# A prompt and sample step of a hybrid layer on one core: idle matmuls at the start, the second layer norm's steps and the samples' sums at other places, and another tail

## The chip, the cores and the metric

The kernel runs on one core of a Trainium2 chip. The metric is the device time of one execution in microseconds (us); lower is better. The kernel before was timed three times: 2386.88, 2387.24 and 2389.86 us, median 2387.24. In the text, PE is TensorE (matmuls), DVE is VectorE, ACT is ScalarE, POOL is GpSimd and SP is SyncE, which here issues most DMAs.

## The reference, cut to what matters

One layer is computed for 2048 prompt tokens and for 64 sample tokens (8 sequences of 8, each with a state of its own). Model width is 1024, the feed-forward width 4096, all in float32.

```python
proj = einsum('btd,dp->btp', x, w_in)                      # 1024 -> 3584
q, f_pre, i_val, g, gate_b, gate_c, h = split(proj, SPLITS)
o, s_new = _hgrn2(silu(q), log_f, k, i_val, s_hgrn)        # 4 heads of 128, chunks of 64
o = o * rsqrt(mean(o * o) + RMS_EPS) * onorm_g * silu(g)
yc = gate_b * conv3(gate_c * h)
mix = einsum('btm,md->btd', concat([o, yc]), w_out)
x = layer_norm(ALPHA * x + mix, ln1_g, ln1_b)
hid = square(relu(einsum('btd,df->btf', x, w_ff1)))        # 1024 -> 4096
x = layer_norm(ALPHA * x + einsum('btf,fd->btd', hid, w_ff2), ln2_g, ln2_b)
```

The outputs are the new tokens of prompt and samples (`y` and `ys`), the heads' states and the last two rows of the convolution's input.

## The kernel before

Matmuls are made in a format with a shorter mantissa. So that the result is as exact as float32, each operand is split into a high part, copied by ACT, and a low part, the difference, made by DVE (L165 for activations, L210 for weights), and each product is three matmuls: high by high, high by low, low by high. The low half isn't made at once: `split` and `unit_split` put it into a list `later`, which `flush` empties, so that DVE's subtraction comes after ACT's copy has been issued. Weights come as units of 128 x 1024 values. SP's queue loads them in the order of use, through three staging buffers `st`, into four pairs `wh`/`wl`; `weights(u)` hands out a unit and splits the ones ahead.

The prompt is worked off in four blocks of 512 tokens, b=0 to 3; the 64 samples go with block 1. A block has these stages, in this order on PE:

- the projections and heads, 56 steps i=0 to 55 (the loop at L862): i=0 to 15 the heads' projections, i=16 to 31 those whose result has tokens on its partitions, i=32 to 55 the convolution's. After each step `rec_step` issues a piece of the heads' recurrence. It is a chain between the engines: DVE builds products and decays (L613, L614, L620, L634, L640), PE makes sums and scores from them (L644, L645, L683, L699), and DVE copies these to their places (L603, L686, L693). A piece comes in the middle of the projections, and on PE its matmuls stand in line with theirs.
- the output projection and the first layer norm.
- the feed-forward part, in two rounds of a first and a second product. It is arranged in the manner of Strassen's method, so that fewer products are needed. In block 0, 64 and later more sums of weight quarters are made by DMAs that POOL issues (`make_sums`, L347 and L349); POOL is started on them by a small addition `tick` (L354). In the second product, the results leave the banks of PSUM by DVE (`add_to`, L1242 and L1245), queued in a list `slow`, one or two of which go into `later` with each unit.
- in block 1, the samples' part of the second product is summed by `sample_sums`. A bank holds two halves of 64 rows; ACT copies the upper one to the lower rows (`upper`, L256), DVE adds the two (L1252), and a third operation adds the sum to the samples' rows (L1259, L1261). The copy and L1252 are issued where `sample_sums` is called, behind the matmuls of that unit, and the third goes into `slow`.

A block's second layer norm is not made at its end. For each tile of 128 tokens (64 for the samples) `layer_norm2` gives three steps, put in a list `bg`: a1, the statistics (L266 twice, L269, L270) and a power by POOL (L271) for one over the deviation; a2, which subtracts the mean and multiplies by the weight (L287); a3, which multiplies by the power, adds the bias (L290) and has POOL store the tile (L291). `pump()` issues the next step of the list. The loop over the next block's 56 steps calls it:

```python
        for i, _ in enumerate(main()):
            rec_step()
            ...
            if i % 2 == 0:
                pump()
        while bg:
            pump()
```

The last block has no next one. Its last part is finished tile by tile (L1374): for each of four tiles PE makes two banks of 512 columns, 12 matmuls each; DVE adds each bank to the tile and takes the statistics, POOL the power; `scaled` (L1363 by DVE, L1364 by ACT) and `stored` (L1370 by DVE, L1371 by POOL, and a DMA) finish the tile before it. The last tile has lines of its own (L1390 to L1398).

What sets the order: each engine takes its instructions in the order in which the program issues them, and waits at each for its operands and buffers. DVE's order is therefore the order of the calls, `flush` and `pump` above.

Of the kernel before, what the change touches and what calls it, by code (L numbers as in the profile page):

```python
# [13 lines left out]
AF = mybir.ActivationFunctionType  # L14
# [3 lines left out]
P = 128  # L18
# [6 lines left out]
NS = 64  # L25
# [36 lines left out]
def hybrid_step(ctx, tc, a, o):  # L62
# [67 lines left out]
    def load_constants():  # L130
        nc.sync.dma_start(small, a["small"])
        nc.sync.dma_start(ident, a["ident"])
        nc.sync.dma_start(mask_f, a["masks"])
        nc.sync.dma_start(smask, a["smask"])
        g.memset(nhalf, -0.5)
        g.memset(halo, 0.0)
        g.memset(ones.bitcast(F32), 1.0)
# [115 lines left out]
    def upper(bank):  # L253

        tmp = TMP().rearrange("p a b -> p (a b)")
        s.activation(tmp[:NS], bank[NS:2 * NS, :], AF.Copy)  # L256
        return tmp[:NS]
# [140 lines left out]
    for _ in range(6):  # L398
        unit_dma()
    load_constants()  # L400
    carry = None


    for b in range(NB):
# [452 lines left out]
        def main():  # L857
            yield from m1()
            yield from m2()
            yield from m3()  # L860

        for i, _ in enumerate(main()):  # L862
            rec_step()
            if b == 0 and i >= 6:
                if i == 6:

                    hold(ks[0][:, 0:1])
                next(making, 0)
                next(making, 0)
            if b == 1 and i % 2 == 0:  # L870
                next(making1, 0)
            if i >= 16 and i % (3 if samp else 4) == 0:
                rec_step()
            if i % 2 == 0:
                pump()
        while bg:
            pump()
# [370 lines left out]

        def sample_sums(bank, into):

            up = upper(bank)
            v.tensor_tensor(up, up, bank[:NS, :], ALU.add)  # L1252

            def add(dh, sign):
                z = x1[NC][:NS, dh * 512:dh * 512 + 512]
                op = ALU.add if sign > 0 else ALU.subtract
                if (NC, dh) in touched:
                    v.tensor_tensor(z, z, up, op)
                else:  # L1259
                    touched.add((NC, dh))  # L1260
                    v.scalar_tensor_tensor(z, z, ALPHA, up, ALU.mult, op)  # L1261

            for dh, sign in into:
                slow.append(lambda dh=dh, sign=sign: add(dh, sign))
# [87 lines left out]
        if b == NB - 1:  # L1352

            c = NCH - 1
            ws = [weights(u) for u in pl["last"]]
            flush_all()
            h, l = last

            sts = [SM((P, 17)) for _ in range(nt)]

            def scaled(t):
                st = sts[t]
                v.scalar_tensor_tensor(st[:, 16:17], st[:, 12:13], -1.0, st[:, 15:16], ALU.mult, ALU.mult)  # L1363
                s.activation(x1[t], x1[t], AF.Identity, scale=st[:, 15:16], bias=st[:, 16:17])  # L1364

            def stored(t):
                for dh in range(2):
                    ds_ = slice(dh * 512, dh * 512 + 512)
                    z = x1[t][:, ds_]
                    v.tensor_tensor(z, z, lnb[:, 0, ds_], ALU.mult)  # L1370
                    g.tensor_tensor(z, z, lnb[:, 1, ds_], ALU.add)  # L1371
                    nc.sync.dma_start(dst(t)[:, ds_], z)

            for t in range(nt):  # L1374
                for dh in range(2):
                    bank = PS()
                    for i in range(FC):
                        slot, cs = 2 * (i // 2) + t // 2, slice(t % 2 * P, t % 2 * P + P)
                        rh, rl = (x[:, (i % 2) * 512:(i % 2 + 1) * 512] for x in ws[2 * dh + i // 2])
                        mm3(bank, h[:, slot, i % 2, cs], l[:, slot, i % 2, cs], rh, rl, i == 0, i == FC - 1)  # L1380
                    if t > 0:
                        if dh == 0:
                            scaled(t - 1)
                        else:
                            stored(t - 1)
                    add_to(t, dh, bank, 1)
                    ln_half(sts[t], x1[t], P, dh)
                ln_rstd(sts[t], P)
            t, st = nt - 1, sts[nt - 1]
            v.scalar_tensor_tensor(st[:, 16:17], st[:, 12:13], -1.0, st[:, 15:16], ALU.mult, ALU.mult)  # L1390
            lo, hi = x1[t][:, :512], x1[t][:, 512:]
            s.activation(lo, lo, AF.Identity, scale=st[:, 15:16], bias=st[:, 16:17])
            v.scalar_tensor_tensor(hi, hi, st[:, 12:13], lnb[:, 0, 512:], ALU.subtract, ALU.mult)
            v.scalar_tensor_tensor(hi, hi, st[:, 15:16], lnb[:, 1, 512:], ALU.mult, ALU.add)
            nc.sync.dma_start(dst(t)[:, 512:], hi)
            v.tensor_tensor(lo, lo, lnb[:, 0, :512], ALU.mult)
            v.tensor_tensor(lo, lo, lnb[:, 1, :512], ALU.add)
            nc.scalar.dma_start(dst(t)[:, :512], lo)  # L1398
        for t in range(nt):
            bg.extend(layer_norm2(x1[t], tsz[t], dst(t)))  # L1400
        x1 = x1g = x1h = x1l = None
# [85 lines left out]
```

## Time and profile before

| | |
|---|---|
| median of three runs | 2387.24 us |
| the profiled execution | 2390.55 us |
| its span | 2388.3 us |
| PE busy | 2340.0 us |
| DVE busy | 1785.6 us |
| ACT busy | 1233.5 us |
| POOL busy | 184.9 us |
| mean granted clock of PE | 0.994 |
| idle time of PE ahead of the first product's `X` | 6.69 us |
| last matmul's end to the end of the span (2379.1 to 2388.3) | 9.2 us |

How to read it: rows give the start and duration in us, the engine, the line, the operation, the tiles out and in (`out<-in`, with buffer numbers left out), their shapes, and how many instructions stand in the row; in brackets the idle time of the engine just before, and which engine's tile and line ended it. A window's row gives its bounds and length, then the busy time of PE, the weight load, DVE, ACT and POOL (with counts), the granted clock of PE, the busy share of the DMA engines, and GB/s. The granted clock is 1.00 at full speed.

By start times, the heads' stage begins at about 612 us in block 1, 1260 in block 2 and 1821 in block 3; the step i=32 of block 3 lies at 1924 us.

### The profile page before, as it was taken

How to read it: one execution, taken by the hardware profiler on the slowest of the kernel's cores; microseconds unless marked ns; L12 is line 12 of the kernel's file. 1: busy time of each engine (PE TensorE's matmuls, PEld its weight loads, DVE VectorE, ACT ScalarE, POOL GpSimd, SP SyncE). 2: the span in 40 equal slices, each digit the busy share in tenths (PEclk: the TensorE clock that was granted, in tenths of full speed). 3: DMA queues.
4: the chain of work that ended last, by engine and by line, in shares of the span. 5: the costliest groups of instructions: out<-in, count | busy, mean ns of one | idle time of the engine just before them, and what ended most of it. 6: DMA issues, size and time to landing. Idle time of an engine off the chain costs nothing.

```text
span 2388.3 us, 38146 instructions
## 1 busy us (share of the span) xinstructions
PE 2340.0 (98%) x15036; PEld 2043.1 (86%) x15036; DVE 1785.6 (75%) x2832; ACT 1233.5 (52%) x1922; POOL 184.9 (8%) x234
## 2 busy tenths in 40 slices
PE   8999999999999999999999999999999999999998
PEld 7778978988879889879878788998988788998996
DVE  7856858578785677875688956888588975888678
ACT  5324645565423446646654234665665324665563
POOL 2230021100101110000000000000000001000001
PEclk9999999999999999999999999999999999999999
DMA  8997598867633644545553325456665325456663
GB/s 285 264 282 214 151 266 273 257 200 211 163 107 78 172 149 133 168 150 177 177 177 109 99 71 194 155 187 197 192 210 163 102 79 172 141 176 203 200 191 119
DMA packets 131507, 418.89 MB, mean 175 GB/s; under 512 B 13376, under 2 KB 17856, under 8 KB 131328
## 3 DMA queue, kind: packets, MB, share of 16 engines
q1 hardware_dynamic: 108880, 347.96, 45.7%
q0 software_dynamic: 22016, 67.71, 11.5%
q8 instruction: 118, 1.93, 0.3%
q10 hardware_dynamic: 432, 0.79, 0.1%
q14 instruction: 61, 0.50, 0.1%
HBM read 405.36 MB, written 69.77 MB: 199 GB/s over the span
## 4 chain that ended last, share of the span: by engine, by line
PE 50%; DVE 5%; DMA 1%; issue 1%; ACT 1%; POOL 0%; POOLq 0%; DVEq 0%; ACTq 0%
PE ps L247 9%; PE ps L245 9%; PE ps L246 9%; PE ps L239 6%; PE ps L240 6%; PE ps L241 6%; DVE wl L210 1%; DMA st<-in_w_ff 1%; PE ps L683 1%; PE ps L250 1%; PE ps L251 1%; DVE S L603 0%; DMA st<-T_b 0%; DVE l L165 0%; ACT wh L203 0%
## 5 line engine op out<-in xcount | busy, mean ns | idle before, releaser
L210 DVE TENSOR_TENSOR wl<-st,wh 128x1024 fp32r<-128x1024 f32 x580 | 707.4, 1221 | 173.3 <-ACT wh L203 171.2
L203 ACT ACTIVATE wh<-st 128x1024 fp32r<-128x1024 f32 x581 | 612.9, 1055 | 352.1 <-PE ps L247 125.6
L239 PE MATMUL ps<-X,wh 128*128 128x256 f32 (+2 forms) x1376 | 466.6, 339 | 9.8 <-ACT X L164 8.3
L240 PE MATMUL ps<-X,wh 128*128 128x256 f32 (+2 forms) x1376 | 456.8, 332 | 0.3 <-DVE X L165 0.3
L241 PE MATMUL ps<-X,wl 128*128 128x256 f32 (+2 forms) x1376 | 456.3, 332 | 0.0
L247 PE MATMUL ps<-wh,l 128*128 128x512 f32 x868 | 340.8, 393 | 9.0 <-DVE l L165 8.6
L245 PE MATMUL ps<-wh,h 128*128 128x512 f32 x868 | 338.2, 390 | 0.0
L246 PE MATMUL ps<-wl,h 128*128 128x512 f32 x868 | 338.0, 389 | 0.0
L239 PEld LDWEIGHTS ps<-X,wh 128*128 128x128 f32 x1376 | 263.0, 191 | 35.0 <-ACT X L164 9.3
L241 PEld LDWEIGHTS ps<-X,wl 128*128 128x128 f32 x1376 | 262.8, 191 | 22.0
L240 PEld LDWEIGHTS ps<-X,wh 128*128 128x128 f32 x1376 | 263.2, 191 | 21.3 <-DVE X L165 1.5
L247 PEld LDWEIGHTS ps<-wh,l 128*128 128x128 f32 x868 | 162.9, 188 | 52.4 <-DVE l L165 19.0
L246 PEld LDWEIGHTS ps<-wl,h 128*128 128x128 f32 x868 | 163.0, 188 | 34.0
L245 PEld LDWEIGHTS ps<-wh,h 128*128 128x128 f32 x868 | 163.0, 188 | 33.1 <-ACT h L164 0.4
L165 DVE TENSOR_TENSOR l<-raw,h 128x512 fp32r<-128x512 f32 x217 | 148.2, 683 | 9.8 <-ACT h L164 9.8
L247 PE MATMUL ps<-X,wl 128*128 128x256 f32 (+1 forms) x528 | 152.1, 288 | 0.2 <-DVE wl L210 0.2
L246 PE MATMUL ps<-X,wh 128*128 128x256 f32 (+1 forms) x528 | 151.9, 288 | 0.0
L245 PE MATMUL ps<-X,wh 128*128 128x256 f32 (+1 forms) x528 | 151.9, 288 | 0.0
L271 POOL TENSOR_TENSOR sm<-sm,nhalf 128x1 f32<-128x1 f32 (+1 forms) x34 | 34.7, 1020 | 1475.8 <-DVE sm L270 1429.6
L1147 DVE TENSOR_TENSOR raw<-raw,ps 128x512 f32<-128x512 f32 (+1 forms) x112 | 61.0, 571 | 104.9 <-PE ps L247 104.7
L164 ACT ACTIVATE h<-raw 128x512 fp32r<-128x512 f32 x217 | 133.7, 616 | 2.3 <-PE ps L246 2.2
L239 PE MATMUL ps<-wh,X 128*128 128x512 f32 x256 | 105.8, 413 | 2.8 <-DVE S L603 2.8
(259 smaller groups left out, 4369.2 us busy)
## 6 DMA issues: line engine op xcount, KB each, us to landing
st<-in_w_ff SPq DMA_DIRECT2D x227, 512.0 KB, 3.7
st<-T_b SPq DMA_DIRECT2D x124, 512.0 KB, 3.7
st<-in_w_in SPq DMA_DIRECT2D x110, 512.0 KB, 3.9
st<-T_a SPq DMA_DIRECT2D x88, 512.0 KB, 3.5
st<-in_w_out SPq DMA_DIRECT2D x56, 512.0 KB, 4.5
T_b<-in_w_ff POOLq DMA_DIRECT2D x48, 512.0 KB, 14.7
T_a<-in_w_ff POOLq DMA_DIRECT2D x36, 512.0 KB, 19.1
T_b<-T_b POOLq DMA_DIRECT2D x16, 512.0 KB, 12.9
```

The costliest lines, as they stand in the source:

```text
L164: s.activation(hi, src, AF.Copy)
L165: later.append(lambda: v.tensor_tensor(lo, src, hi.bitcast(F32), ALU.subtract))
L203: s.activation(wh, st, AF.Copy)
L210: v.tensor_tensor(wl, st, wh.bitcast(F32), ALU.subtract)
L239: te.matmul(out, lh, rh, start=first, stop=False)
L240: te.matmul(out, lh, rl, start=False, stop=False)
L241: te.matmul(out, ll, rh, start=False, stop=last)
L245: te.matmul(out, lh, rh, start=first, stop=False, skip_group_check=True)
L246: te.matmul(out, lh, rl, start=False, stop=False, skip_group_check=True)
L247: te.matmul(out, ll, rh, start=False, stop=last, skip_group_check=True)
L271: g.tensor_tensor(st[:n, 15:16], st[:n, 14:15], nhalf[:n, 0:1], ALU.pow)
L1147: v.tensor_tensor(z, z, ps, (ALU.add, ALU.subtract)[op - 2])
```

## The change

It has four parts.

1. Ahead of the first block, PE makes twelve matmuls of 128 x 512 on the tile `ones`, into a bank that nobody reads.
2. `pump()` is called at other steps. `first_steps` is six in block 1, three in block 2 and none in block 3; so many steps of the second layer norm are issued at i=2, 5, 8 and so on, and the rest at the even i from 26 on.
3. In `sample_sums` the copy goes into `later`, and L1252's add into `slow`, ahead of the third operation.
4. In the tail, `stored` adds the bias by DVE instead of POOL, and the last tile is finished by four DVE operations on halves, two without and two with the power, with no ACT step.

```diff
     load_constants()
+
+    idle = PS((P, 4, P))
+    for _ in range(12):
+        te.matmul(idle, ones, ones.unsqueeze(1).to_broadcast([P, 4, P]), start=True, stop=True)
+    idle = None
...
+        first_steps = 3 * max(0, len(bg) // 3 + nt + (1 if samp else 0) - 8)
+
         for i, _ in enumerate(main()):
...
-            if i % 2 == 0:
+            if i % 3 == 2 and first_steps:
+                first_steps -= 1
+                pump()
+            elif i >= 26 and i % 2 == 0:
                 pump()
...
         def sample_sums(bank, into):
-            up = upper(bank)
-            v.tensor_tensor(up, up, bank[:NS, :], ALU.add)
+            up = []
+            later.append(lambda: up.append(upper(bank)))
+            slow.append(lambda: v.tensor_tensor(up[0], up[0], bank[:NS, :], ALU.add))
...
-                    v.tensor_tensor(z, z, up, op)
+                    v.tensor_tensor(z, z, up[0], op)
...
-                    v.scalar_tensor_tensor(z, z, ALPHA, up, ALU.mult, op)
+                    v.scalar_tensor_tensor(z, z, ALPHA, up[0], ALU.mult, op)
...
                     v.tensor_tensor(z, z, lnb[:, 0, ds_], ALU.mult)
-                    g.tensor_tensor(z, z, lnb[:, 1, ds_], ALU.add)
+                    v.tensor_tensor(z, z, lnb[:, 1, ds_], ALU.add)
                     nc.sync.dma_start(dst(t)[:, ds_], z)
...
             t, st = nt - 1, sts[nt - 1]
-            v.scalar_tensor_tensor(st[:, 16:17], st[:, 12:13], -1.0, st[:, 15:16], ALU.mult, ALU.mult)
-            lo, hi = x1[t][:, :512], x1[t][:, 512:]
-            s.activation(lo, lo, AF.Identity, scale=st[:, 15:16], bias=st[:, 16:17])
-            v.scalar_tensor_tensor(hi, hi, st[:, 12:13], lnb[:, 0, 512:], ALU.subtract, ALU.mult)
-            v.scalar_tensor_tensor(hi, hi, st[:, 15:16], lnb[:, 1, 512:], ALU.mult, ALU.add)
-            nc.sync.dma_start(dst(t)[:, 512:], hi)
-            v.tensor_tensor(lo, lo, lnb[:, 0, :512], ALU.mult)
-            v.tensor_tensor(lo, lo, lnb[:, 1, :512], ALU.add)
-            nc.scalar.dma_start(dst(t)[:, :512], lo)
+            halves = [slice(dh * 512, dh * 512 + 512) for dh in range(2)]
+            for ds_ in halves:
+                z = x1[t][:, ds_]
+                v.scalar_tensor_tensor(z, z, st[:, 12:13], lnb[:, 0, ds_], ALU.subtract, ALU.mult)
+            for ds_, queue_ in zip(halves, (nc.sync, nc.scalar)):
+                z = x1[t][:, ds_]
+                v.scalar_tensor_tensor(z, z, st[:, 15:16], lnb[:, 1, ds_], ALU.mult, ALU.add)
+                queue_.dma_start(dst(t)[:, ds_], z)
```

PE's order is otherwise the same, and so is ACT's. In the rows below, names carry the numbers of their buffers, and the lines of the kernel after are those of the one before plus 5 in the heads' stage and plus 11 to 12 from `sample_sums` on.

The first place is DVE's order in block 3's heads, where L603 fills a bank's place for the head's sums (a row at 1896 us in the trace). Before:

```order
L620 TENSOR_TENSOR S_17916<-S_17916 128x8
L287 SCALAR_TENSOR_TENSOR tok_14270<-tok_14270,sm_18359,lnb 128x1024
L693 COPY_PREDICATED S_18023<-masks,ps_18442 32x4x2x8 x4
L613 TENSOR_TENSOR S_17912<-S_17912,S_18024 128x32x8
L614 TENSOR_TENSOR S_17961<-S_17961,S_18024 128x32x8
L620 TENSOR_TENSOR S_18024<-S_18024 128x32
L210 TENSOR_TENSOR wl_18466<-st_18392,wh_18394 128x1024
L640 TENSOR_TENSOR S_18487<-S_18380,S_18382 128x512
L603 COPY_PREDICATED S_18187<-masks,ps_18484 128x256
L290 SCALAR_TENSOR_TENSOR tok_14270<-tok_14270,sm_18359,lnb 128x1024
L634 TENSOR_TENSOR S_18504<-S_18151,S_18208 128x256
```

And now the same stretch:

```order
L625 TENSOR_TENSOR S_17920<-S_17920 128x8
L698 COPY_PREDICATED S_18020<-masks,ps_18421 32x4x2x8 x4
L618 TENSOR_TENSOR S_17916<-S_17916,S_18021 128x32x8
L619 TENSOR_TENSOR S_17959<-S_17959,S_18021 128x32x8
L625 TENSOR_TENSOR S_18021<-S_18021 128x32
L210 TENSOR_TENSOR wl_18445<-st_18372,wh_18374 128x1024
L645 TENSOR_TENSOR S_18466<-S_18360,S_18362 128x512
L608 COPY_PREDICATED S_18176<-masks,ps_18463 128x256
L639 TENSOR_TENSOR S_18481<-S_18140,S_18196 128x256
```

The last tile's L287 and L290 are gone from here, as are the steps of the three tiles before it; nothing else moved.

The second place is DVE's order in the same block some 45 us later, at i=34 (in the trace before, from 1934.6 us on), where the convolution's first operations come in (L532, L535, L541). Before:

```order
L210 TENSOR_TENSOR wl_18895<-st_18814,wh_18816 128x1024
L693 COPY_PREDICATED S_18408<-masks,ps_18914 32x4x2x8 x4
L613 TENSOR_TENSOR S_18151<-S_18151,S_18409 128x32x8
L614 TENSOR_TENSOR S_18208<-S_18208,S_18409 128x32x8
L620 TENSOR_TENSOR S_18409<-S_18409 128x32
L532 COPY S_18950<-halo 128x2
L535 TENSOR_TENSOR S_18950<-ps_18901,S_18879 128x512
L541 COPY halo<-S_18950 128x2
L686 COPY S_18187<-ps_18956 64x4x64
```

And now the same stretch:

```order
L210 TENSOR_TENSOR wl_18887<-st_18800,wh_18802 128x1024
L698 COPY_PREDICATED S_18388<-masks,ps_18906 32x4x2x8 x4
L618 TENSOR_TENSOR S_18140<-S_18140,S_18389 128x32x8
L619 TENSOR_TENSOR S_18196<-S_18196,S_18389 128x32x8
L625 TENSOR_TENSOR S_18389<-S_18389 128x32
L287 SCALAR_TENSOR_TENSOR tok_14130<-tok_14130,sm_18853,lnb 128x1024
L537 COPY S_18943<-halo 128x2
L540 TENSOR_TENSOR S_18943<-ps_18893,S_18871 128x512
L546 COPY halo<-S_18943 128x2
L691 COPY S_18176<-ps_18949 64x4x64
```

A tile's L287 came in ahead of the convolution's first operations. Its statistics (L266 twice, L269, L270) stand seven rows further up, ahead of the L686 that started at 1933.27 us in the trace before, and its L290 some eleven rows further down. Block 2 has the same picture.

The third place is DVE's order in block 1's second product, around the first L1252 (1004.93 us in the trace before). Before:

```order
L210 TENSOR_TENSOR wl_9936<-st_9911,wh_9913 128x1024
L1234 SCALAR_TENSOR_TENSOR raw_9227<-raw_9227 128x512
L165 TENSOR_TENSOR l_9916<-raw_8585,h_9915 128x512
L165 TENSOR_TENSOR hp_9918<-tok_8945,hp_9918 128x2x64
L1252 TENSOR_TENSOR tmp_9966<-tmp_9966,ps_9870 64x512
L210 TENSOR_TENSOR wl_9969<-st_9941,wh_9943 128x1024
L1234 SCALAR_TENSOR_TENSOR raw_9489<-raw_9489 128x512
```

And now:

```order
L165 TENSOR_TENSOR hp_9931<-tok_8958,hp_9931 128x2x64
L210 TENSOR_TENSOR wl_9979<-st_9954,wh_9956 128x1024
L1245 SCALAR_TENSOR_TENSOR raw_9502<-raw_9502 128x512
L165 TENSOR_TENSOR l_9959<-raw_8767,h_9958 128x512
L165 TENSOR_TENSOR hp_9961<-tok_8958,hp_9961 128x2x64
L210 TENSOR_TENSOR wl_10014<-st_9986,wh_9988 128x1024
L1256 SCALAR_TENSOR_TENSOR tok_8334<-tok_8334,ps_9869 128x512
L1256 SCALAR_TENSOR_TENSOR tok_8336<-tok_8336,ps_9870 128x512
L165 TENSOR_TENSOR l_9991<-raw_9240,h_9990 128x512
L165 TENSOR_TENSOR hp_9993<-tok_8958,hp_9993 128x2x64
L210 TENSOR_TENSOR wl_10045<-st_10020,wh_10022 128x1024
L1264 TENSOR_TENSOR tmp_9984<-tmp_9984,ps_9883 64x512
```

The add (now L1264) no longer stands ahead of the next unit's L210, but behind the L210 of two units later; one unit's splits (L165 twice) and two adds of results (now L1256) lie between.

## The prediction

> **What bounds the kernel now.** I read the page first, then the list of waits, then TensorE's (PE's) rows at its own gaps, and last the rows of the engine that each gap waited for.
>
> ```profile
> PE 2340.0 (98%) x15036; PEld 2043.1 (86%) x15036; DVE 1785.6 (75%) x2832; ACT 1233.5 (52%) x1922; POOL 184.9 (8%) x234
> ```
>
> PE is busy for 2340.0 of 2388.3 us, so the time is PE's work plus PE's gaps, and only 48.3 us are not PE's. The change takes no matmul away (it adds twelve at the start); what it can win or lose is gaps, stretches of low clock, and the tail behind the last matmul. The gaps that concern it are in the heads' stage of blocks 2 and 3, in block 1's feed-forward part, at the start, and in the tail.
>
> The heads' stage. The rows are windows of 20 us (busy time of PE, weight load, VectorE (DVE), ScalarE (ACT), GpSimd (POOL), then the granted clock), PE's rows at the gaps of block 2 and of block 3, and DVE's rows ahead of block 3's gaps.
>
> ```profile
> 1330.00:1350.00 20.00, 17.26 (x127) 13.25 (x126) 18.32 (x45) 4.37 (x7) 1.13 (x2) 0.83 0.26 89
> 1892.00:1912.00 20.00, 17.26 (x142) 13.40 (x141) 19.54 (x46) 6.08 (x10) 0.57 (x1) 1.00 0.32 107
> ...
> 1334.04 0.39 PE L241 MATMUL ps<-wh,X 128*128 128x512 f32 x1
> 1335.81 0.50 PE L239 MATMUL ps<-wh,X 128*128 128x512 f32 x1 [1.38 <-DVE S L603]
> 1338.13 1.70 PE L683 MATMUL ps<-S,S 128*64 128x64 f32 x40 [1.35 <-ACT tok L506]
> 1342.07 0.63 PE L241 MATMUL ps<-wh,X 128*128 128x512 f32 x1
> ...
> 1897.04 0.50 PE L239 MATMUL ps<-wh,X 128*128 128x512 f32 x1 [1.38 <-DVE S L603]
> 1899.37 1.07 PE L683 MATMUL ps<-S,S 128*64 128x64 f32 x40 [1.36 <-ACT tok L506]
> ...
> 1883.38 1.28 DVE L266 BATCH_NORM_STATS2 sm<-tok 128x6 f32<-128x512 f32 x2
> 1891.35 1.28 DVE L287 SCALAR_TENSOR_TENSOR tok<-tok,sm,lnb 128x1024 f32<-128x1024 f32 x1
> 1896.27 0.72 DVE L603 COPY_PREDICATED S<-masks,ps 128x256 f32<-128x256 uint8 x1
> 1896.80 1.25 DVE L290 SCALAR_TENSOR_TENSOR tok<-tok,sm,lnb 128x1024 f32<-128x1024 f32 x1
> ```
>
> DVE works 19.54 of 20 us here, so it is DVE that is late, and four of its operations in this stretch (L266 twice, L287, L290, with two small ones some 4.05 us from start to start) are the previous block's second layer norm, which nobody on PE waits for. L603 stands behind them; PE needs its bank at 1897.04 and sits. The second gap is the same lateness by way of ACT, whose copies L506 stand behind an ACT step that needs the next DVE product. Block 2 shows the same pair.
>
> Block 1's second feed-forward product. The first row is from the list of waits (us in total, times, longest), then one of its eight cases, the PE row behind it, and the two stretches that hold all eight.
>
> ```profile
> DVE tmp L1252 <- ACT tmp L256: 32.6, 8, 5.0
> ...
> 1004.93 0.68 DVE L1252 TENSOR_TENSOR tmp<-tmp,ps 64x512 f32<-64x512 f32 x1 [4.38 <-ACT tmp L256]
> ...
> 1008.30 0.47 PE L250 MATMUL ps<-wh,hp 128*128 128x512 f32 x1 [1.31 <-DVE hp L165]
> ...
> 1000.00:1056.00 56.00, 53.44 (x231) 42.68 (x230) 42.82 (x65) 28.54 (x44) 0.00 (x0) 1.00 0.43 142
> 1186.00:1242.00 56.00, 53.46 (x232) 42.66 (x231) 45.30 (x67) 29.61 (x45) 0.00 (x0) 1.00 0.51 162
> ```
>
> DVE stands still for 4.38 us although it has work behind L1252: that add needs a copy of a bank which PE is still filling, and DVE takes its work in order. Afterwards the weight's low half L210, a row sum L1234 and the splits L165 come late, and PE waits for `hp`. PE misses 56.00 - 53.44 = 2.56 us in one stretch and 2.54 in the other.
>
> **The change, part by part.** Sums are made against the profiled execution (2390.55 us, of which 2388.3 are the span); it lies 3.31 above the median of the runs, 2387.24, so the result is moved to that median at the end.
>
> *Idle matmuls.* PE's first rows, then POOL's chain in block 0:
>
> ```profile
> 6.69 0.80 PE L239 MATMUL ps<-X,wh 128*128 128x512 f32 x1 [6.69 <-ACT X L164]
> ...
> 12.20 0.63 PE L240 MATMUL ps<-X,wh 128*128 128x512 f32 x1
> 12.63 0.63 PE L241 MATMUL ps<-X,wl 128*128 128x512 f32 x1
> ...
> 13.44 0.39 PE L240 MATMUL ps<-X,wh 128*128 128x512 f32 x1
> 13.67 0.40 PE L241 MATMUL ps<-X,wl 128*128 128x512 f32 x1
> ...
> 24.08 0.70 POOL L354 TENSOR_TENSOR tick<-S 128x1 f32<-128x1 f32 x1 [23.06 <-ACT S L466]
> ...
> 172.91 2.52 POOL L720 TENSOR_TENSOR sm<-sm,nhalf 128x4 f32<-128x4 f32 x2
> ...
> 176.41 0.66 PE L729 MATMUL ps<-ident,S 128*128 128x128 f32 x4 [3.09 <-DVE S L725]
> ...
> 100.00:176.00 76.00, 73.32 (x576) 60.06 (x574) 44.43 (x112) 21.17 (x47) 24.27 (x32) 1.00 1.05 290
> ```
>
> The first matmuls stand 0.43 us apart, from 13.44 on 0.23: the clock is low until then. Twelve idle ones cost 12 x 0.43 = 5.2 us from about 1 us on (`ones` is one of the first tiles written) and end at about 6.2, inside the 6.69 that PE waits anyway. If the clock is then up, the eight or ten matmuls between 8.75 and 13.06 win 0.2 each, some 2.0 us. That isn't kept: at 176.41 PE waits 3.09 us for a chain that leads back to POOL (L720 at 172.91), which had spent the time since its `tick` at 24.08 on transfers, at a DMA share of 1.05. PE's lead runs into this wait, save for the part by which the `tick` comes sooner and full DMA queues let it through. Ends 0 and -2.0; nearest to the saturated row I take **-0.5**.
> The Trainium skill (TensorE: Matmul & The Clock Gate, "What's actually happening") says that the budget is about 3.4 us of busy time in a window that runs free, so that twelve idle matmuls may or may not fill a window; the trace has the low clock for 13.06 - 6.69 = 6.4 us of sparse matmuls, and no run here shows yet what dense ones do. By the page the term would be 0 in some runs and -0.5 in others.
>
> *Second layer norm later.* Before, a tile's three steps stood at the even steps from i=0; now blocks 1 and 2 run six and three steps early, block 3 none, and the rest from i=26 on. In blocks 2 and 3 the operations are no longer ahead of L603. DVE's lag at 1896 is at most some 5 us (the layer norm's operations of the last two tiles alone are 8.1), so both gaps should go in both blocks. From start to start a gap costs a little more than its idle time (1335.81 - 1334.04 - 0.23 = 1.54 for 1.38 us), so 3.0 us a block for the two. In block 2 the clock also fell: after the second gap twelve matmuls stand 0.43 apart with 0.63 each, as at 1342.07, 12 x 0.2 = 2.35 us. Block 3's equal gaps brought no such drop (granted clock 1.00 against 0.83). Gone: 3.0 + 2.35 + 3.0 = 8.35 us.
> By the same section of the Trainium skill the clock falls after an idle window of about 3.4 us; here it fell after two gaps of 1.4 us within 4 us, so the measured rows count. By the page alone the 2.35 us would not belong to these gaps, and the whole sum would come out that much later (the second case of the clock's rival below).
>
> What comes late instead is seen where the steps stand now, i=32 to 36 of blocks 2 and 3. DVE's idle times there in block 3, and the PE rows that take its results:
>
> ```profile
> 1938.11 0.69 DVE L535 TENSOR_TENSOR S<-ps,S 128x512 f32<-128x512 f32 x1 [0.35 <-PE ps L241]
> 1939.58 0.41 DVE L614 TENSOR_TENSOR S<-S,S 128x256 f32<-128x256 f32 x1
> 1943.86 0.42 DVE L614 TENSOR_TENSOR S<-S,S 128x256 f32<-128x256 f32 x1
> 1945.31 0.69 DVE L559 TENSOR_TENSOR S<-ps,S 128x512 f32<-128x512 f32 x1 [0.95 <-PE ps L241]
> 1958.18 0.69 DVE L535 TENSOR_TENSOR S<-ps,S 128x512 f32<-128x512 f32 x1 [6.58 <-PE ps L241]
> ...
> 1941.87 0.66 PE L699 MATMUL ps<-ident,S 128*128 128x128 f32 x4
> 1945.20 0.45 PE L683 MATMUL ps<-S,S 128*32 128x32 f32 x16
> ```
>
> At i=32 the statistics (1.28 for L266 twice, and some 0.35 of small operations) and at i=34 L287 (1.2 from start to start) come ahead of the L614 that ends at 1939.99: 2.8 less the 0.35 idle is 2.5 us late. PE's L699 has 1941.87 - 1939.99 = 1.88 us in hand: it waits 0.6. The next L614 ends at 1944.28, 0.92 ahead of its L683: 2.5 late, less 0.92, less the 0.6 already lost: another 0.95. Then 0.95 and 6.58 us of idle time take up L290 and the rest; the steps from i=42 on fall into such idle time. So +1.55 us in each of two blocks; by bounds from 0 (DVE had run ahead) to 6.8 (see the rivals). In block 1 DVE has idle time at the new places and no gap was due to the old ones: 0. Together -8.35 + 3.1 = **-5.2**, ends -8.4 and +10.0.
>
> *The samples' sums.* L1252 goes into the list of late work and comes out behind the next unit's split, when the copy has long been made. The eight waits of DVE fall away, with them 2.56 + 2.54 us of gaps, and 0.16 for each of eight restarts as above: 6.4. No DVE work is added. The bank that it reads is held one step longer, and by the code six of eight are in use there. **-6.4**, ends -6.9 and -4.5.
>
> *The tail.*
>
> ```profile
> 2371.10 0.16 DVE L1363 SCALAR_TENSOR_TENSOR sm<-sm 128x1 f32<-128x1 f32 x1 [1.00 <-POOL sm L271]
> 2372.58 1.29 DVE L1370 TENSOR_TENSOR tok<-tok,lnb 128x512 f32<-128x512 f32 x2
> 2376.81 0.16 DVE L1363 SCALAR_TENSOR_TENSOR sm<-sm 128x1 f32<-128x1 f32 x1 [1.18 <-POOL sm L271]
> 2382.47 0.16 DVE L1390 SCALAR_TENSOR_TENSOR sm<-sm 128x1 f32<-128x1 f32 x1 [1.13 <-POOL sm L271]
> 2383.33 0.75 DVE L1394 SCALAR_TENSOR_TENSOR tok<-tok,sm,lnb 128x512 f32<-128x512 f32 x1
> 2384.72 0.69 DVE L1397 TENSOR_TENSOR tok<-tok,lnb 128x512 f32<-128x512 f32 x1
> ```
>
> A tile takes 2376.81 - 2371.10 = 5.71 us, above PE's 24 x 0.23 = 5.44, so DVE with POOL's power is the limit. Three tiles get two more DVE operations, each dependent on the one before it and so 0.72 apart: 3 x 1.44 = +4.3. POOL, rid of its adds, answers the power sooner, 0.73 as for the first tile instead of 1.00 and 1.18: -0.7. For the last tile the wait of 1.13 now lies beside two operations that need no power, and four operations (0.67 apart, 0.75 the last) take 2.7 us from the statistics' end at 2381.34 where 2385.41 - 2381.34 = 4.07 stood: -1.4. **+2.2**, ends -1.2 (PE hides the added work) and +2.9 (no faster power).
>
> Sum: -0.5 - 5.2 - 6.4 + 2.2 = -9.9, so 2380.6 for an execution like the profiled one and **2377.3 us** against the median.
>
> **Rivals.**
> - *No new gaps.* DVE enters the late steps without its old lag, and its layer norm fits beside PE's slack: the 3.1 goes, and with some of the start kept the sum is -13 to -15: 2373. For it: 2.22 us of idle DVE just ahead of 1924.27, which my layout leaves unused. Against: DVE can't run ahead of the banks that PE fills.
> - *The clock.* The new gaps (0.6 and 0.95) bring a drop like block 2's, 2.35 in each block: -9.9 + 4.7 = -5.2, 2382.0. Or block 2's drop belongs to the place and stays: -7.5, 2379.7. For it: equal gaps brought it in one block and not in the other.
> - *The other side.* DVE becomes the bound at i=32 to 40 of blocks 2 and 3: the 6.8 us that the layer norm inserts there all reach PE, once per block, because every PE row waits for the L614 before it. 13.6 instead of 3.1, and a drop of 2.35 in each: -9.9 + 10.5 + 4.7 = +5.3, 2392.5. It decides when DVE is late by more than the 0.92 to 1.88 us in hand at every step in a row; against it stand the 0.95 and 6.58 us of idle time.
> - *The idle matmuls do nothing* (the clock falls again before 8.75, or POOL's chain takes it all): 0 for -0.5, 2377.8, within the forecast.
>
> **How the numbers follow.** Forecast, with the idle matmuls' rival in it (2374.5 to 2380), 0.52; no new gaps (down to 2370) 0.17; the clock, or one large term half as large as thought (2380 to 2386), 0.22; the other side 0.05; a loss at a place not seen that takes most of the gain (2386 to 2392) 0.04. The range for 8 in 10 goes from 2371 to 2384. A measurement of this kernel tells about 0.2% (4.8 us) from no change, so faster means below 2382.5: 0.52 + 0.17 and nearly half of the 0.22, 0.79; the same up to 2392: 0.12 + 0.04 = 0.16; slower 0.05.
>
> **What would show it.** Right: no gaps of PE at 1008, 1024, 1051 and their three counterparts of the second stretch, DVE's L1252 without idle time ahead of it; no gap at L603 and ahead of L683 in blocks 2 and 3, granted clock 1.00 there, and short new gaps 30 to 50 us further on; the wait at block 0's L729 longer by about 1.5; a tail of 6.7 us per tile whose last DVE operation ends some 2 us later behind the last matmul. Wrong: gaps of over 2 us at i=32 to 40, a granted clock below 1.00 there, DVE idle at L1252 still, or a tail as short as before.

## The result

| | before | changed |
|---|---|---|
| runs beside the first timing | 2387.68 us, median of 6 | 2378.05 us, median of 6 |
| ratio to before, without the execution of 3249.48 us | | 0.9943 (95% interval 0.9928 to 0.9959) |
| runs beside the experiments | 2391.12 us, median of 29 | 2378.33 us, median of 5 |
| ratio to before | | 0.9948 (0.9935 to 0.9960) |
| span of the profiled execution | 2388.3 us | 2378.5 us |

The change makes the kernel about 0.5% faster; forecast were 2377.3 us and a gain of 9.9. One of the first six runs, the profiled one, took 3249.48 us at a mean granted clock of 0.658, so the median of the other five, 2377.19 us, is what to compare, and the profile shown here is that of another execution of the same kernel (e1). Its lines are those of the changed kernel: L608 is the old L603, L619 the old L614, L688 and L704 the old L683 and L699, L734 the old L729, L1264 the old L1252, L1375 the old L1363; L1406 and L1409 are the last tile's four operations, L404 the idle matmuls.

PE's line of the page, then the windows that answer to those shown of before: the two stretches of the samples' sums, and the places in blocks 2 and 3 where L603 had been late.

```profile
PE 2339.3 (98%) x15048; PEld 2046.1 (86%) x15048; DVE 1791.1 (75%) x2837; ACT 1232.5 (52%) x1921; POOL 178.9 (8%) x228
...
1002.00:1058.00 56.00, 56.00 (x249) 46.37 (x248) 47.05 (x69) 31.16 (x48) 0.00 (x0) 1.00 0.51 161
1184.00:1240.00 56.00, 56.00 (x249) 46.39 (x248) 50.09 (x73) 32.05 (x48) 0.00 (x0) 1.00 0.57 182
1324.00:1344.00 20.00, 20.00 (x200) 15.81 (x198) 16.52 (x41) 6.55 (x10) 1.42 (x1) 1.00 0.26 80
1882.00:1902.00 20.00, 20.00 (x199) 15.86 (x198) 16.51 (x43) 6.56 (x10) 1.41 (x1) 1.00 0.26 83
```

PE is busy in the whole of all four. At the old places of the layer norm DVE has fallen from 18.3 and 19.5 busy us in 20 to 16.5, and the granted clock is 1.00 in both blocks. The only new gaps of PE in the heads' stage stand further on, in block 2 and in block 3; with them, DVE's two operations of the layer norm that lie ahead of block 3's:

```profile
1372.17 0.66 PE L704 MATMUL ps<-ident,S 128*128 128x128 f32 x4 [0.49 <-DVE S L619]
1376.54 0.45 PE L688 MATMUL ps<-S,S 128*32 128x32 f32 x16 [0.94 <-DVE S L625]
1929.01 0.66 PE L704 MATMUL ps<-ident,S 128*128 128x128 f32 x4 [0.49 <-DVE S L619]
1933.39 0.45 PE L688 MATMUL ps<-S,S 128*32 128x32 f32 x16 [0.96 <-DVE S L625]
...
1919.61 1.28 DVE L266 BATCH_NORM_STATS2 sm<-tok 128x6 f32<-128x512 f32 x2
1925.69 1.28 DVE L287 SCALAR_TENSOR_TENSOR tok<-tok,sm,lnb 128x1024 f32<-128x1024 f32 x1
```

The gaps are 0.49 and 0.94 to 0.96 us, behind the statistics and L287, at the two rows for which 0.6 and 0.95 had been worked out. The second waits for L625 (the old L620), the operation right behind the L614 that the prediction named. In block 1's heads' stage a pair of gaps of 1.02 and 0.44 us stands near 710 us; it is the same in all 13 traces compared here, with the old order, the new one and without L290 (e11). The tail, DVE's rows: the scale of tiles 2 and 3, then the last tile from the end of its statistics.

```profile
2360.24 0.16 DVE L1375 SCALAR_TENSOR_TENSOR sm<-sm 128x1 f32<-128x1 f32 x1 [0.72 <-POOL sm L271]
2366.93 0.16 DVE L1375 SCALAR_TENSOR_TENSOR sm<-sm 128x1 f32<-128x1 f32 x1 [0.72 <-POOL sm L271]
2372.75 0.15 DVE L270 TENSOR_SCALAR sm<-sm 128x1 f32<-128x1 f32 x1
2372.82 1.41 DVE L1406 SCALAR_TENSOR_TENSOR tok<-tok,sm,lnb 128x512 f32<-128x512 f32 x2
2374.14 1.41 DVE L1409 SCALAR_TENSOR_TENSOR tok<-tok,sm,lnb 128x512 f32<-128x512 f32 x2
```

A tile takes 2366.93 - 2360.24 = 6.69 us (5.71 before), POOL's power is waited for 0.72 (1.00 and 1.18), and the last tile needs 2375.55 - 2372.90 = 2.65 us from the statistics' end.

The add of the samples' sums hardly makes DVE wait any more. The row of e1's list of waits that answers to L1252's (us in total, times, longest):

```profile
DVE tmp L1264 <- ACT tmp L256: 0.7, 2, 0.4
```

In all eight cases together it was 32.6 us.

Because PE's order is the same in all these kernels but for the idle matmuls, the time between two given matmuls can be compared from trace to trace. Each row is a stretch of PE's work, named by its times in the trace before; the numbers are the difference to that trace in us.

| stretch of before | e1 (all) | e2 sums | e3 layer norm | e4 tail | e5 idle matmuls | e8 last tile |
|---|---|---|---|---|---|---|
| first matmul to 16 | -3.07 | -1.80 | -1.98 | -1.69 | -3.09 | -1.52 |
| 180 to 610 (block 0) | +7.14 | +4.15 | +8.25 | +2.71 | +8.47 | +5.49 |
| 700 to 720 | -1.52 | -1.51 | -1.51 | -1.51 | -1.51 | +0.01 |
| 990 to 1056 (sums) | -3.97 | -3.97 | -0.01 | -0.03 | -0.03 | +0.03 |
| 1186 to 1242 (sums) | -3.99 | -3.99 | -0.03 | -0.04 | -0.05 | -0.03 |
| 1320 to 1350 (block 2) | -5.96 | -0.14 | -5.96 | +0.04 | -0.04 | -2.84 |
| 1370 to 1400 (block 2) | +1.61 | 0.00 | +1.61 | 0.00 | 0.00 | 0.00 |
| 1880 to 1910 (block 3) | -3.11 | +1.51 | -3.11 | +0.03 | +0.01 | +1.45 |
| 1910 to 1960 (block 3) | +1.59 | 0.00 | +1.61 | 0.00 | 0.00 | 0.00 |
| last matmul to the end | +2.01 | +0.01 | +0.01 | +2.02 | +0.02 | -0.91 |

What an edit moves repeats to some 0.02 us. Other stretches move by themselves: block 0 by up to 10 us, 1320 to 1350 by 2.8, and 700 to 720 and 1880 to 1910 by 1.5. So do some that the table leaves out: 16 to 180 by up to 4.0 us, 720 to 990 by 1.5, 1400 to 1880 by up to 1.7, others by 0.6 or less. In the stretches of 700 to 990, 1320 to 1350 and 1880 to 1910 it is the granted clock that drops in some executions (see the last section).

### The profile page after: what moved, and what is told of

Its sections match the earlier page's. It is cut to its first block, busy times and chain, and to the rows that moved or that the text cites. A ratio compares the mean times of both kernels' runs of the same rounds, so it can differ in the third digit from the quotient of the medians.

```text
span 3247.7 us, 38159 instructions
## 1 busy us (share of the span) xinstructions
PE 3236.5 (100%) x15048; PEld 2463.3 (76%) x15048; DVE 1806.6 (56%) x2837; ACT 1242.4 (38%) x1921; POOL 178.9 (6%) x228
## 4 chain that ended last, share of the span: by engine, by line
PE 99%; DVE 0%; DMA 0%; issue 0%; DVEq 0%; ACT 0%; SPq 0%
PE ps L239 16%; PE ps L240 15%; PE ps L241 15%; PE ps L245 15%; PE ps L247 15%; PE ps L246 15%; PE ps L688 1%; PE ps L250 1%; PE ps L251 1%; PE ps L917 1%; PE ps L779 1%; PE ps L751 1%; PE ps L782 1%; PE ps L649 0%; PE ps L650 0%; PE ps L827 0%
## 5 line engine op out<-in xcount | busy, mean ns | idle before, releaser
L210 DVE TENSOR_TENSOR wl<-st,wh 128x1024 fp32r<-128x1024 f32 x580 | 708.9, 1222 | 499.3 <-ACT wh L203 498.7
L239 PE MATMUL ps<-X,wh 128*128 128x256 f32 (+2 forms) x1376 | 578.1, 420 | 1.7 <-DVE S L608 1.0
L240 PE MATMUL ps<-X,wh 128*128 128x256 f32 (+2 forms) x1376 | 570.5, 415 | 0.3 <-DVE X L165 0.3
L241 PE MATMUL ps<-X,wl 128*128 128x256 f32 (+2 forms) x1376 | 569.9, 414 | 0.0
L247 PE MATMUL ps<-wh,l 128*128 128x512 f32 x868 | 435.8, 502 | 0.0
L245 PE MATMUL ps<-wh,h 128*128 128x512 f32 x868 | 435.3, 502 | 0.0
L246 PE MATMUL ps<-wl,h 128*128 128x512 f32 x868 | 435.3, 502 | 0.0
L239 PEld LDWEIGHTS ps<-X,wh 128*128 128x128 f32 x1376 | 308.8, 224 | 68.7 <-issue 23.6
L240 PEld LDWEIGHTS ps<-X,wh 128*128 128x128 f32 x1376 | 312.1, 227 | 60.9 <-issue 19.7
L241 PEld LDWEIGHTS ps<-X,wl 128*128 128x128 f32 x1376 | 308.6, 224 | 62.6 <-issue 19.5
L246 PE MATMUL ps<-X,wh 128*128 128x256 f32 (+1 forms) x528 | 184.1, 349 | 0.0
L247 PE MATMUL ps<-X,wl 128*128 128x256 f32 (+1 forms) x528 | 183.7, 348 | 0.0
L245 PE MATMUL ps<-X,wh 128*128 128x256 f32 (+1 forms) x528 | 183.6, 348 | 0.0
L165 DVE TENSOR_TENSOR l<-raw,h 128x512 fp32r<-128x512 f32 x217 | 148.5, 684 | 41.7 <-ACT h L164 41.5
L239 PE MATMUL ps<-wh,X 128*128 128x512 f32 x256 | 131.5, 514 | 0.0
```

The costliest lines, as they stand in the source:

```text
L165: later.append(lambda: v.tensor_tensor(lo, src, hi.bitcast(F32), ALU.subtract))
L210: v.tensor_tensor(wl, st, wh.bitcast(F32), ALU.subtract)
L239: te.matmul(out, lh, rh, start=first, stop=False)
L240: te.matmul(out, lh, rl, start=False, stop=False)
L241: te.matmul(out, ll, rh, start=False, stop=last)
L245: te.matmul(out, lh, rh, start=first, stop=False, skip_group_check=True)
```

## The experiments

**e1, the changed kernel again.**

> The changed kernel as it is, for a profile at full clock. Theory (the prediction's sum): 9 to 11 us below the kernel before, PE without gaps at the eight sums of the samples and at L608 (the old L603) in blocks 2 and 3, new gaps of 0.6 and 0.95 us at i=34 to 36 of both blocks, the granted clock 1.00 there, the wait at block 0's L734 (the old L729) longer by about 1.5 us, a tail of 6.7 us per tile. Rival (no new gaps): 13 to 15 us below, no gap of over 0.3 us at i=32 to 40. Rival (clock): about 5 us below, with a granted clock under 0.95 in a window of 20 us of block 2 or 3.

Measured above: 12.4 us below (0.0052 of 2391.12; 9.6 to 15.5 by the interval), in the traces 9.8. The theory's gaps, period and tail came as worked out; the clock's rival and that of no new gaps fell. One thing did not come as expected: the wait at block 0's L734.

```profile
1.07 4.98 PE L404 MATMUL ps<-ones 128*128 128x512 f32 x12 [1.07 <-POOL ones L137]
6.97 0.50 PE L239 MATMUL ps<-X,wh 128*128 128x512 f32 x1 [0.92 <-ACT X L164]
...
172.63 1.12 PE L734 MATMUL ps<-ident,S 128*128 128x128 f32 x4 [2.11 <-DVE S L730]
```

The idle matmuls lie in PE's wait, and the first real one takes 0.50 us instead of 0.80. But the wait at L734 is 2.11 us, not longer but shorter than the 3.09 of before. One pair of traces says little here: the same wait is between 0 and 3.09 us in the eight traces without idle matmuls and between 0.14 and 2.11 in the five with them.

**e2 to e4, one part each.** e2 takes over the edit of `sample_sums`, e3 that of `first_steps` and `pump`, e4 that of `stored` and the last tile, each as in the diff above and alone.

> The kernel before with the samples' sums alone moved. Theory: 6.4 us faster, DVE without the idle times of 3.8 to 4.4 us ahead of the add, PE without gaps in the two stretches of 56 us (5.1 us of gaps before). Rival (the wait only moves): the add, now behind the late work, delays the bank's release or the row sums, and less than half of it, under 3.2 us, is left.

2382.74 us, ratio 0.9968 (0.9958 to 0.9978): 7.7 us faster. Windows of the two stretches in e2:

```profile
997.00:1053.00 56.00, 56.00 (x248) 46.37 (x248) 47.29 (x70) 30.13 (x46) 0.00 (x0) 1.00 0.49 160
1180.00:1236.00 56.00, 56.00 (x249) 46.39 (x248) 49.83 (x72) 32.15 (x49) 0.00 (x0) 1.00 0.57 184
```

No gap is left, and the stretches are 3.97 and 3.99 us shorter. The rival falls.

> The kernel before with the second layer norm's steps alone moved. Theory: 5.2 us faster: 8.35 us of gaps and low clock gone in blocks 2 and 3, 1.55 us of new gaps in each. Rival (no new gaps): 8.4 us faster. Rival (DVE the bound at i=32 to 40): slower by 5 to 10 us, with gaps of over 2 us there.

2385.60 us, ratio 0.9984 (0.9974 to 0.9995): 3.8 us faster (1.2 to 6.2). The traces give -5.96 + 1.61 - 3.11 + 1.61 = -5.85 us in blocks 2 and 3, of which part is the clock (below). PE's new gaps in block 2 of e3:

```profile
1382.90 0.66 PE L699 MATMUL ps<-ident,S 128*128 128x128 f32 x4 [0.49 <-DVE S L614]
1387.28 0.45 PE L683 MATMUL ps<-S,S 128*32 128x32 f32 x16 [0.94 <-DVE S L620]
```

They are the same as in e1 to 0.01 us, so they belong to this part alone. Both rivals fall.

> The kernel before with the new tail alone. Theory: 2.2 us slower, a tile's period 6.7 us instead of 5.71, the last DVE operation ending about 2.2 us later behind the last bank's add's old place (2385.4 us of the span before). Rival (PE or the waits for POOL hide the added operations): no slower than before, up to 1.2 us faster.

2392.40 us, ratio 1.0009 (0.9999 to 1.0019): +2.2 us, by time alone not told from nothing. In the trace the end lies 2.02 us further behind the last matmul, as in e1 (2.01). The rival falls.

**e5, the idle matmuls alone** (the first hunk of the diff).

> The kernel before with the twelve idle matmuls alone. Theory: the first unit ends some 2 us sooner, PE's wait at block 0's L729 grows by what was won, and at most 0.9 us sooner is left at its end; the time is the same within 1 us. Rival (the lead is kept): 1.5 to 2 us faster, the chain from POOL's tick to L729 having moved by as much.

2389.60 us, ratio 0.9998 (0.9989 to 1.0006). Counted from its first matmul, the first unit ends 3.09 us sooner than in the trace before, but 1.5 to 2.0 us of that come without idle matmuls too in e2, e3, e4 and e8 (the table's first row), and 0.7 to 0.8 in e10 to e12: how long the low clock lasts at the start varies. Of the lead nothing is left at 610 us: that point is reached at 613.0 us, and between 606.0 and 615.8 in the eight executions of kernels without idle matmuls (the kernel before, e2 to e4, e8, e10 to e12). By time alone, theory and rival can't be told apart: the interval goes from 2.6 us faster to 1.4 slower. The traces speak for the theory's amount, but not for its way. The matmul at 180 us, behind the wait at L734, comes at 175.15 us in the mean of the five executions with idle matmuls and at 177.25 in the mean of the eight without, so a lead of about 2 us is still there; at 610 the means are 612.3 and 610.9. In the five executions with idle matmuls the stretch from 180 to 610 took 435.4 to 438.4 us, in the eight without 428.5 to 438.2.

**e6, the changed kernel with the old tail** (the last two hunks of the diff undone).

> The changed kernel with the old tail. Theory: 2.0 us faster than the changed kernel, some 14 us below the kernel before, everything ahead of the tail as in the changed kernel. Rival (the loss of the tail is made up elsewhere): the same as the changed kernel.

2376.88 us, ratio 0.9948 (0.9935 to 0.9961); in the trace the end lies +0.01 us behind the last matmul against before, and +2.01 in e1. By time the gain of 2 isn't told from nothing (e1's ratio is the same), by the trace it is plain.

**e7, no step at i=32 to 40, and the last tile alone.**

```diff
-            elif i >= 26 and i % 2 == 0:
+            elif i in (26, 28, 30) or i >= 42:
...
-                    v.tensor_tensor(z, z, lnb[:, 1, ds_], ALU.add)
+                    g.tensor_tensor(z, z, lnb[:, 1, ds_], ALU.add)
```

> The changed kernel with two edits: in the heads' stage no step of the second layer norm between i=32 and i=40 (late ones at i=26, 28, 30 and at every i from 42), and of the new tail only the last tile's four DVE operations, the bias of the others by POOL as before. Theory: the gaps of 0.5 and 0.95 us at i=34 to 36 go in blocks 2 and 3 (3.2 us), and the tail is 1.4 us shorter than the old one: some 6 to 7 us faster than the changed kernel. Rival (DVE's idle time at i=42 to 55 doesn't take nine steps): new gaps behind i=42 of the same size or larger, and nothing won but the tail.

2373.74 us, ratio 0.9932 (0.9920 to 0.9944). The gaps at L704 and L688 are gone in both blocks, but another came, in part as the rival had it:

```profile
1974.36 0.65 PE L734 MATMUL ps<-ident,S 128*128 128x128 f32 x4 [1.07 <-DVE S L730]
```

Nine steps of layer norm now stand between i=42 and i=50, and the gap is 1.07 us in each block (1.2 us longer stretches). It isn't that DVE has no room for nine steps: it is idle for 4.64 us shortly before, ahead of L540, in both blocks. But one L290 stands between the two L730 that PE waits for here (e9 below shows the rows). So of the 3.2 us 0.8 are won, and 2.92 in the tail: 3.7 us, where 6 to 7 were expected.

**e8, the last tile alone**, in the kernel before.

> The kernel before with the last tile's four DVE operations alone, the bias of the other tiles by POOL as before. Theory: the last DVE operation ends 2.7 us behind the statistics instead of 4.07, so 1.4 us faster. Rival (the DMAs' landing sets the end, or the two operations ahead of the power delay it): no faster.

2389.46 us, ratio 1.0000 (0.9990 to 1.0010); in the trace the end comes 0.91 us sooner, less than the 1.4 expected. POOL's and DVE's rows at the end of e8 show why:

```profile
2379.36 2.81 POOL L1371 TENSOR_TENSOR tok<-tok,lnb 128x512 f32<-128x512 f32 x2 [2.33 <-PE ps L241]
2381.51 1.88 DVE L1393 SCALAR_TENSOR_TENSOR tok<-tok,sm,lnb 128x512 f32<-128x512 f32 x2
2382.14 0.99 POOL L271 TENSOR_TENSOR sm<-sm,nhalf 128x1 f32<-128x1 f32 x1
```

The first two operations take 1.88 us where the same pair takes 1.41 in e1, and POOL's power 0.99, where it took 0.55 in the kernel before and 0.92 in e1. DVE's pair begins while POOL still adds the third tile's bias (until 2382.17). e12 tests that.

**e9 and e10, two tiles early in every block**; e10 without the idle matmuls.

```diff
-        first_steps = 3 * max(0, len(bg) // 3 + nt + (1 if samp else 0) - 8)
+        first_steps = 6 if b else 0
```

> The kernel of e7 with two tiles of the second layer norm early (i=2 to 17) in blocks 2 and 3 as in block 1, so that fewer steps are left for i=42 and later (nine in e7's block 2 and 3; six and three here). Theory: at L603's place (now L608) DVE's lag is still gone, since the last early step lies 20 us ahead; the gap of 1.07 us that e7 has at L734 in blocks 2 and 3 shrinks to under 0.4; 1.5 to 2.3 us faster than e7, some 18 us below the kernel before. Rival (any early tile brings the lag back): gaps at L608 and ahead of L688 again, 3 us or more in each block, slower than e7.

2375.27 us, ratio 0.9935 (0.9921 to 0.9950), by time not told from e7. In the trace block 3 has no gap any more (its stretch from 1960 on is 1.2 us shorter than e7's), and no gap came back at L608 in blocks 2 and 3. Block 2 kept its 1.07 at L734, though only six of the nine steps are left there, as expected. DVE's rows ahead of it:

```profile
1414.22 0.69 DVE L540 TENSOR_TENSOR S<-ps,S 128x512 f32<-128x512 f32 x1 [4.66 <-PE ps L241]
1415.70 1.27 DVE L290 SCALAR_TENSOR_TENSOR tok<-tok,sm,lnb 64x1024 f32<-64x1024 f32 x1
1419.47 0.68 DVE L730 TENSOR_TENSOR S<-S,tok 128x512 f32<-128x512 f32 x1
```

L290, the last of the six steps, stands between two L730 (at 1415.03 and 1419.47), and PE's L734 at 1420.21 waits for the second. In block 3 the last of three late steps is L290 at 1957.90, no step stands between the two L730, and there is no gap. So the theory holds for block 3; in block 2 the place of one step counts, not the number of steps. A version that keeps this place free in block 2 was not run.

> The kernel of e9 without the idle matmuls. Theory (the lead is lost at block 0's wait): the same as e9 within 1 us. Rival (the lead is kept): 1.5 to 3 us slower than e9.

2374.19 us, ratio 0.9941 (0.9926 to 0.9955): 1.1 us less than e9 in the median, 1.4 more by the ratios. The rival's 1.5 to 3 more lie within the intervals, so this run shows no gain of the idle matmuls and can't rule out a small one.

**e11, the kernel before without L290** (its line is taken out of `layer_norm2`; lines below it move up by one).

> The kernel before without L290, the third step's operation on DVE, in the second layer norm of blocks 0 to 2 (the output lacks its scale and bias); POOL's power and its store stay at their places. Theory (DVE's own lag makes the gaps): in block 3 one L290 of 1.2 us lies ahead of L603 and two ahead of the second gap, so the first gap falls from 1.38 to about 0.2 us and the second from 1.36 to 0. Rival (POOL's powers and stores, or PE's own order, make them): both gaps stay within 0.2 us.

One execution, 2385.24 us. PE's rows at the two gaps of block 3:

```profile
1892.80 0.50 PE L239 MATMUL ps<-wh,X 128*128 128x512 f32 x1 [0.21 <-DVE S L602]
1893.99 1.07 PE L682 MATMUL ps<-S,S 128*64 128x64 f32 x40 [0.22 <-ACT tok L505]
```

The first gap fell from 1.38 to 0.21 us, by the length of one L290, though POOL's powers and stores stayed. DVE's lag makes the gaps. The second fell to 0.22, not to 0; in block 2 they are 0.21 and 0.21.

**e12, e8 without POOL's last addition.**

```diff
-                    g.tensor_tensor(z, z, lnb[:, 1, ds_], ALU.add)
+                    if t < nt - 2 or dh == 0:
+                        g.tensor_tensor(z, z, lnb[:, 1, ds_], ALU.add)
```

> The kernel of e8 without the last addition that POOL makes, the bias of the second half of the third tile, which is left out of the output. Theory (POOL's addition and DVE's operations with two tiles from SBUF shut each other out): the last tile's first DVE operation takes 0.74 us again instead of 1.22, and the last DVE operation ends 1.4 us sooner than in the kernel before, counted from the statistics. Rival (the operation was slow for another reason): it still takes over 1.1 us.

One execution, 2381.92 us. DVE's and POOL's rows at the end:

```profile
2374.26 1.41 DVE L1394 SCALAR_TENSOR_TENSOR tok<-tok,sm,lnb 128x512 f32<-128x512 f32 x2
2374.49 0.92 POOL L271 TENSOR_TENSOR sm<-sm,nhalf 128x1 f32<-128x1 f32 x1 [0.78 <-DVE sm L270]
2375.58 1.41 DVE L1397 SCALAR_TENSOR_TENSOR tok<-tok,sm,lnb 128x512 f32<-128x512 f32 x2
```

The pair takes 1.41 us again, and the end comes 1.37 us sooner than in the kernel before. The theory holds. POOL's power, which starts inside DVE's first operation, still takes 0.92, as in e1 and e4.

## Why the prediction was right

- **The sum** was 9.9 us; measured were 10.5 (the first medians, 2387.68 less 2377.19), 13.6 (the first ratio; 9.8 to 17.2), 12.4 (the ratio beside the experiments; 9.6 to 15.5) and 9.8 (the two traces). Added up from the stretches, the parts come to -7.96 - 5.85 + 2.01 = -11.8, so the forecast was some 2 us short. That the two traces give 9.8 is luck: block 0 alone moves by 10 us from execution to execution, and in e1 it was 7.14 slower from 180 to 610.
- **The samples' sums** were the largest term and were mis-sized: -6.4 forecast, -7.96 in the traces. The gaps were all there; what each restart costs beside its gap was put at 0.16 us and is some 0.27, since the second matmul behind a gap is issued 0.11 late as well (0.34 us behind the first, where 0.23 is usual), and PE was late at ten places, not eight, some of them with gaps of 0.1 us or none.
- **The layer norm** was right in mechanism and size: the lag goes (e11 shows that DVE's own lag made the gaps), both gaps vanish in both blocks, and new ones of 0.49 and 0.94 us came where 0.6 and 0.95 were worked out from DVE's idle time and PE's slack. Net -5.2 forecast, -5.85 in the traces. Block 2's 5.96 holds a drop of the clock worth 2.84 us (e8 has the same gaps there without it), put at 2.35. The drop did come from the gaps: of the six profiled executions that keep them (before, e2, e4, e5, e8, e12) five have it in block 2 and two in block 3, and none of the seven without them has one at either place. That block 3 was counted without a drop fits the trace before and not every execution.
- **The tail**: +2.2 forecast, +2.01 measured; 6.7 per tile forecast, 6.69 measured. PE's 24 x 0.23 us for a tile are 5.52, not 5.44 (which goes with 0.227); both are under the 5.71, so nothing hangs on it.
- **The idle matmuls**: -0.5 forecast, nothing measurable found. The amount stands, the place was wrong: it was said that the wait at block 0's L729 would take up the lead and grow by 1.5 us. No trace shows that: about 2 us of lead are still there at 180 us, behind this wait, which varies by 3 us by itself. The lead is gone by 610 us, in block 0's feed-forward part, whose own waits vary by more than the lead. Which of them takes it up stays open.
- Of the rivals, that of no new gaps and that of the other side fell with the rows at L704 and L688; the clock's, as a drop behind the new gaps, was not seen in e1, e3 or e6, and as a drop that belongs to the place and stays, in none of the seven executions without the old gaps.

A version that beats both kernels in the trace is e9's schedule with the last tile's four operations and POOL's bias, with or without idle matmuls. Against e1 it has 2.0 us less for the new gaps (3.20 less 1.15 at block 2's L734) and 2.9 us less in the tail. By its ratio (0.9935) it is not told from the changed kernel (0.9943 and 0.9948).

## What to carry to other kernels

An operation that must wait, issued into an engine's line ahead of work that is ready, costs the ready work's time; moving it behind that work is nearly free, and the bank that it holds longer has to be counted. Background work on a busy engine is best placed by the idle time between two rows on which the bound engine waits: that sum, made by hand from the trace, gave e1's gaps right to some 0.1 us. Where it wasn't made, at L734 in e7 and e9, a gap of 1.07 us came although the engine had idle time enough nearby. Where one stage varies by itself, compare the others from trace to trace between the same two instructions; effects of 1 us show there that the total time hides.

## What the runs showed of the hardware

**Whether two gaps bring a drop of the clock depends on where they fall in windows of 3.41 us.** In each of the 13 traces compared, the changes of PE's clock lie whole multiples of 3.413 us apart: in the trace before, 628.05 us (184 times 3.413) lie between the drops at 709.70 and 1337.75. Where this grid lies differs from execution to execution. The kernel before and e8 have the same code in blocks 2 and 3 and the same gaps of 1.3 to 1.4 us. These are windows on each trace's grid, the kernel before first and e8 second: in each, those that hold the gaps of block 2 and the one or two behind them, then the same for block 3.

```profile
1334.34:1337.75 3.41, 1.05 (x4) 0.49 (x3) 3.38 (x7) 0.57 (x2) 0.57 (x1) 1.00 0.53 154
1337.75:1344.58 6.83, 6.45 (x51) 5.27 (x52) 6.40 (x19) 2.74 (x5) 0.14 (x1) 0.50 0.43 156
1894.13:1897.54 3.41, 2.03 (x9) 1.40 (x8) 3.38 (x6) 0.00 (x0) 0.00 (x0) 1.00 0.27 47
1897.54:1900.95 3.41, 2.05 (x46) 1.42 (x45) 3.41 (x7) 2.54 (x6) 0.57 (x1) 1.00 0.63 253
1900.95:1904.36 3.41, 3.41 (x46) 2.58 (x45) 3.31 (x13) 1.66 (x2) 0.00 (x0) 1.00 0.56 166
...
1335.42:1338.83 3.41, 1.87 (x7) 0.88 (x6) 3.38 (x5) 0.00 (x0) 0.00 (x0) 1.00 0.42 114
1338.83:1342.25 3.42, 2.23 (x45) 1.93 (x46) 3.42 (x8) 3.18 (x6) 0.57 (x1) 1.00 0.49 198
1342.25:1345.66 3.41, 3.41 (x46) 2.53 (x45) 3.34 (x12) 1.19 (x2) 0.00 (x0) 1.00 0.56 154
1895.20:1898.61 3.41, 1.42 (x10) 0.94 (x11) 3.41 (x7) 1.41 (x4) 0.57 (x1) 1.00 0.52 154
1898.61:1902.03 3.42, 3.42 (x42) 2.76 (x41) 3.35 (x11) 1.91 (x3) 0.00 (x0) 0.50 0.62 216
```

Where most of the two gaps lies in one window (PE busy for 1.05 and 1.42 us of it), the clock is 0.50 for the next one or two windows. Where a border lies between the gaps (2.03 and 2.05, 1.87 and 2.23), it stays at 1.00. The six executions with these gaps have twelve such pairs: seven brought a drop, behind a window with 1.01 to 1.70 us of busy PE, and five brought none, with 1.87 us or more. At these places it is chance where the grid lies, and the rest follows from it. Elsewhere the bound is less sharp: a window with 1.95 us brought the drop at 709.70 in the trace before, and one with 1.63 us, from 457.11 on, brought none.

The two gaps cost 3.1 us, and with a drop 1.5 us (one window) or 2.8 us (two) more. The Trainium skill (TensorE: Matmul & The Clock Gate, "What's actually happening") has a window of about 3.4 us that runs free of the kernel, which agrees with the 3.41 us here. By its table the clock falls after an idle window of about 3.4 us; here a window with up to 1.70 us of busy PE was enough.

**POOL and DVE shut each other out.** While POOL added two tiles from SBUF, a DVE operation with two tiles from SBUF took longer (the pair 1.88 us against 1.41), and POOL's power, started inside such an operation, 0.92 us instead of 0.54 (e1, e4 and e12). The Trainium skill (SBUF — State Buffer, "SBUF: two separate sides") says that a DVE operation with two inputs from SBUF and a POOL operation that reads SBUF hold a common port each for its whole length, and that the other one blocks; e8 and e12 agree. The prediction took the last tile's operations at their undisturbed length, which holds in the changed kernel only because POOL has nothing left to add. POOL's power took 0.92 us there too, but DVE had its second operation to do meanwhile: the power ended at 2373.97, and L1409 began at 2374.14.
